# Picking silu and its product ahead of weight copies in the feed-forward parts of a two-layer decoder trunk

## The chip, the cores and the metric

The kernel runs on one core of one Trainium2 chip. The metric is the device time of one execution in microseconds (us). The core's engines are named as in the profile: PE does matrix products and PEld their weight loads, ACT the activations and copies, DVE the elementwise work, POOL a few small operations, and SP issues the loads from HBM.

## The reference

Two layers (D = 1024, 256 positions, so two tiles of 128 positions, called t = 0 and t = 1) each mix tokens by attention and then run a SwiGLU feed-forward part, all in float32. The change touches only the second half of each layer:

```
h = rms_norm(x, norm_ffn[l]) * (1.0 + sc_f) + sh_f
gt, up = jnp.split(h @ w_ffn_in[l], 2, axis=-1)
x = x + g_f * ((jax.nn.silu(gt) * up) @ w_ffn_out[l])
```

The inner width of the feed-forward part, D_FF, is 2816.

## The kernel before

Every float32 weight is used as two parts. A weight tile of 1 MB (128 x 2048) is loaded from HBM into a buffer called `raw`. ACT copies it with rounding into `hi`, DVE subtracts (`raw - hi`) into `lo`, and each product of activations with weights is then three matmuls on PE: hi by hi, hi by lo, lo by hi. There are three `raw` buffers for this stage, and three `hi` and three `lo`; a new copy into `hi` can start only when the last matmul that reads the buffer's old contents has been issued and done.

The feed-forward part (stage `ffn`, function `sublayer_ffn`) goes through D_FF in six blocks: five of 512 columns and one of 256. For each block and each t, PE gathers the gate sums in one bank of the matmul memory (tiles called `bank`) and the up sums in another. Then `post` runs: ACT takes silu of the gate bank into a `tmp` tile, DVE multiplies it by the up bank, PE transposes the product, and ACT and DVE split the transposed product into a high and a low part (`aT`). The silu frees the gate bank for new sums, the product frees the up bank. Six banks hold such sums. The second product (stage `fout`) follows: eleven tiles of `w_ffn_out` are loaded, split in the same way and multiplied with `aT` into four banks.

The order of instructions on each engine isn't written out by hand. `Program.order` plans it before the kernel is built: it walks through time with estimated costs, and among the operations that can start at about the same moment on an engine it picks the one of highest rank. The rank is the length of the work that hangs on the operation plus a boost; operations recorded inside `with R.ahead():` get 1000 on top on every engine but PE, which puts them before all others that are ready:

```
def rank(self, e):
    return self.level + self.boost + (FIRST if self.first and e != "PE" else 0.0)
```

The split of weights (`split_unit`, line 631 for the copies and line 583 for the subtractions) is recorded inside such a block, `post` is not. Where the plan expects PE to wait for over 1.4 us, `fill` puts matmuls with a tile of zeros (`zb`, line 456) into the wait; their result is not used. PE takes its instructions in the planned order, and so do ACT, DVE and SP.

Of the kernel before, what the change touches and what calls it, by code (L numbers as in the profile page):

```python
# [8 lines left out]
F32 = mybir.dt.float32  # L9
# [3 lines left out]
AF = mybir.ActivationFunctionType  # L13
ALU = mybir.AluOpType
# [93 lines left out]
def AP(x):  # L108
    return x.ap() if isinstance(x, Ref) else x


def cols(x):
    n = 1
    for d in AP(x).shape[1:]:
        n *= d
    return n
# [442 lines left out]
class Engines:  # L559
# [22 lines left out]
    def tt(self, out, a, b, op, engs=("DVE",)):  # L582
        self._vec(engs, cols(out), True, lambda v: v.tensor_tensor(AP(out), AP(a), AP(b), op=op), [a, b], [out])  # L583
# [31 lines left out]
    def act(self, out, a, func, scale=None, bias=None, accum=None, late=()):  # L615
        kw, reads = {}, [a]
        c = (0.17 if self._psum(a) else 0.215) + cols(out) / 1200
        if scale is not None:
            kw["scale"] = scale
            reads.append(scale)  # L620
            c += 0.08 if isinstance(scale, Ref) else 0.0
        if bias is not None:
            kw["bias"] = bias
            reads.append(bias)
            c += 0.08
        writes = [out]
        if accum is not None:
            kw["accum_out"] = accum
            writes.append(accum)
            c += 0.2  # L630
        op = self.p.op({"ACT": (c, [lambda: self.nc.scalar.activation(AP(out), AP(a), func,  # L631
                                                                      **{k: AP(x) for k, x in kw.items()})])},
                       reads + list(late), writes)
        if any(func in x for x in TABLES):
            op.func = func
# [32 lines left out]
    def tr(self, out, a, ident):  # L668
        self.p.op({"PE": (0.109, [lambda: self.nc.tensor.transpose(AP(out), AP(a), AP(ident))])}, [a, ident], [out])  # L669

    def dma(self, out, src, q="SP", least=60000):
        o = AP(out)
        n = SIZE[o.dtype]
        for d in o.shape:
            n *= d
        n = max(n, least)
        eng = {"SP": self.nc.sync, "POOL": self.nc.gpsimd}[q]
        return self.p.op({q: (0.43 if q == "SP" else 0.6, [lambda: eng.dma_start(AP(out), AP(src))])},  # L678
                         [src], [out], nbytes=n)
# [5 lines left out]


HALVED = 1
SPILL = [("kb",), ("kb",)]
SPILL_FIRST = True
ADA_PACE = [(1.5, 1.5, 1.0), (0.7, 0.7, 0.3)]  # L690
# [11 lines left out]
def trunk_kernel(tc, pools, A):  # L702
# [14 lines left out]
    R = Program(nc)  # L717
    E_ = Engines(R)
    tt, stt, ttr, ts, act, evac, mm, tr, dma = (E_.tt, E_.stt, E_.ttr, E_.ts, E_.act, E_.evac, E_.mm, E_.tr, E_.dma)
# [46 lines left out]
    def temp(n=512):  # L766
        return R.val("tmp", lambda a: a[:, :n])
# [54 lines left out]
    def ada_dot(w, col):  # L822
        stt(w, w, 0.5, crow, ALU.mult, ALU.mult, accum=col)
# [303 lines left out]
    def lead_in(bs, h, W):  # L1127
# [7 lines left out]
        def load(k):  # L1135
            adas[k] = R.val("sa")
            src = A["w_ada"][0, :2 * D].rearrange("(j k p) c -> p j k c", j=2, p=P)[:, :, k]
            dst = adas[k].rearrange("p (j c) -> p j c", j=2)
            for js in ((slice(0, 1), slice(1, 2)) if k < HALVED else (slice(0, 2),)):
                dma(dst.of(js.start)[:, js] if k < HALVED else dst, src[:, js])  # L1140
            raws[k] = R.val("raw", lambda a: a[:, :NC0])
# [44 lines left out]
        for k in range(KD):  # L1186
# [3 lines left out]
            for j in range(2):  # L1190
                ada_dot((adas[k].of(j) if k < HALVED else adas[k])[:, j * D:(j + 1) * D], mod.of(k)[:, j, k:k + 1])
            with R.ahead():
# [20 lines left out]
    def sublayer_mix(l, h):  # L1213
# [355 lines left out]
        else:  # L1569
# [10 lines left out]
            for t in range(NT):  # L1580
                post_grpA(t, b1[t], b2[t])
            dense(0, 512, spilled(post_qa, SP["qa"]) if "qa" in SPILL[l] else post_qa)
        PACE[0] = ADA_PACE[l][0]
        mlp()
        if l:
            dense(1304, 512, spilled(post_qb, SP["qb"]) if "qb" in SPILL[l] else post_qb)
        dense(1816, 512, spilled(post_kb, SP["kb"]) if "kb" in SPILL[l] else post_kb)
        dense(2328, 512, post_vb)
# [57 lines left out]
    def sublayer_ffn(l, h):  # L1646
        W = A["w_ffn_in"][l]
        R.stage = f"{l}ffn"
        aT = {t: [] for t in range(NT)}
        last = [None]  # L1650

        def post(t, n, bg, bu):
            th = temp(n)
            act(th, bg[:, :n], AF.Silu)
            tt(th, th, bu[:, :n], ALU.mult)
            bt = R.val("t")
            with R.burst():
                for k in range(n // P):
                    tr(bt[:, k * P:(k + 1) * P], th[:, k * P:(k + 1) * P], ident)
            if t == 0:  # L1660
                last[0] = R.val("aT", dt=F32R)
            hi, lo = (quarter(last[0], 2 * t + i, t, i)[:, :n] for i in range(2))
            act(hi, bt[:, :n], AF.Copy)
            tt(lo, bt[:, :n], hi.bitcast(F32), ALU.subtract)
            aT[t] += [(hi[:, j * P:(j + 1) * P], lo[:, j * P:(j + 1) * P]) for j in range(n // P)]

        PACE[0] = ADA_PACE[l][2]
        c0 = 0
        while c0 < DFF:
            n = min(512, DFF - c0)  # L1670
            kt = 2048 // n
            nu = KD // kt
            b = {}
            us = {}
            for w, i in ([("gu"[c], k) for c, k, t in FFN_TURNS if t == 0] if c0 == 0 else
                         [(w, i) for w in "gu" for i in range(nu)]):
                off = c0 + (DFF if w == "u" else 0)
                us[w, i] = load_unit(W[i * kt * P:(i + 1) * kt * P, off:off + n], kt, n, spare=c0 == 0)
            keys = [(w, i, t) for w in "gu" for i in range(nu) for t in range(NT)]
            if c0 == 0:  # L1680
                keys = [("gu"[c], i, t) for c, i, t in FFN_TURNS]
            for w, i, t in keys:
                if i == 0:
                    b[w, t] = R.val("n")
                part(b[w, t], h[t], us[w, i], i * kt, i == 0)
            for t in range(NT):
                post(t, n, b["g", t], b["u", t])
            c0 += n

        WO = A["w_ffn_out"][l]  # L1690
        R.stage = f"{l}fout"
        R.boost = 100.0 if l == L - 1 else 0.0
        gate(l, "g_f")
        R.boost = 0.0
        nu = KF // 2
        bs = {(t, c): R.val("n") for t in range(NT) for c in range(2)}
        us = []
        for i in range(nu):
            ada_pace(PACE[0])
            raw = R.val("raw")  # L1700
            dma(raw.rearrange("p (k n) -> p k n", k=2), WO[i * 256:(i + 1) * 256].rearrange("(k p) n -> p k n", p=P))
            us.append(split_unit(raw, 2, D, l < L - 1 and i >= nu - 4))
        nl = 3 if l == L - 1 else 4
        keys = [(i, t, k, c) for i in range(nu - nl) for t in range(NT) for k in range(2) for c in range(2)]
        full = (0, 512)
        keys = [(*key, full) for key in keys]

        parts = {(t, c): [full] for t in range(NT) for c in range(2)}
        if l == L - 1:
            parts[(NT - 1, 1)] = [(0, 256), (256, 512)]  # L1710
            keys += [(i, t, k, c, e) for t in range(NT) for c in range(2) for e in parts[(t, c)]
                     for i in range(nu - nl, nu) for k in range(2)]
        else:
            keys += [(i, t, k, c, full) for t in range(NT) for i in range(nu - nl, nu) for k in range(2) for c in range(2)]
        for i, t, k, c, (e0, e1) in keys:
            kk = 2 * i + k
            cs_ = slice(c * 512 + e0, c * 512 + e1)
            b = bs[(t, c)]
            if (e0, e1) != full:
                b = b.of(e0)[:, e0:e1]  # L1720

            R.boost = 20.0 * (4 - 2 * t - c) - e0 / 50 if l == L - 1 and i >= nu - nl else 0.0
            mm3(b, aT[t][kk], us[i].hi[:, k, cs_], us[i].lo[:, k, cs_], kk == 0)
        R.boost = 0.0
        hn = []
        if l < L - 1:
            log_soon(last)
        for t in range(NT):
            for c in range(2):
                if l < L - 1:  # L1730
                    resid(l, t, c, bs[(t, c)], ada[l]["g_f"])
                    continue
                for e0, e1 in parts[(t, c)]:
                    xx = resid(l, t, c, bs[(t, c)], ada[l]["g_f"], e0, e1)
                    dma(out[t * P:(t + 1) * P, c * 512 + e0:c * 512 + e1], xx)
            if l < L - 1:
                hn.append(h_chain(t, *modulation(l + 1, "m")))
        return hn
# [58 lines left out]
```

## Time and profile before

| what | value |
|---|---|
| median of 3 runs | 827.29 us (824.45 to 827.35) |
| the profiled execution's own time | 825.58 us |
| its span in the profile | 823.8 us |
| PE busy, share of the span | 98% |
| DVE busy | 70% |
| ACT busy | 50% |

The span is what the profile covers from the first instruction to the last; the profiled execution's own time lies 1.8 us above it. In rows of the timeline a line stands for neighbouring instructions of one kind: start, duration, engine, line, operation, result and operands, shapes, their number, and in brackets how long the engine stood idle ahead of them and what ended the wait. Buffer numbers are left out there. The ends of matmuls are modelled and overlap the next start, so the pace of PE is read from start to start.

### The profile page before, as it was taken

How to read it: one execution, taken by the hardware profiler on the slowest of the kernel's cores; microseconds unless marked ns; L12 is line 12 of the kernel's file. 1: busy time of each engine (PE TensorE's matmuls, PEld its weight loads, DVE VectorE, ACT ScalarE, POOL GpSimd, SP SyncE). 2: the span in 40 equal slices, each digit the busy share in tenths (PEclk: the TensorE clock that was granted, in tenths of full speed). 3: DMA queues.
4: the chain of work that ended last, by engine and by line, in shares of the span. 5: the costliest groups of instructions: out<-in, count | busy, mean ns of one | idle time of the engine just before them, and what ended most of it. 6: DMA issues, size and time to landing. Idle time of an engine off the chain costs nothing.

```text
span 823.8 us, 10564 instructions
## 1 busy us (share of the span) xinstructions
PE 807.9 (98%) x4008; PEld 611.3 (74%) x4008; DVE 580.3 (70%) x1025; ACT 410.7 (50%) x654; POOL 79.6 (10%) x75
## 2 busy tenths in 40 slices
PE   8999999999999999999999999999999999998997
PEld 4567656754878888888878877775487888886886
DVE  6879876777887878776888897775468353444544
ACT  5455366652673334533684647576257353342431
POOL 4703620000100000000000360000000000000000
PEclk9999999999999999999999999999999999999999
DMA  9967585449858887967854876340473545644341
GB/s 358 416 241 266 179 297 189 153 130 333 328 192 320 316 323 269 340 261 282 314 188 174 309 245 215 141 155 1 178 281 122 186 151 207 204 153 154 142 165 51
DMA packets 74018, 183.82 MB, mean 223 GB/s; under 512 B 4304, under 2 KB 9696, under 8 KB 73456
## 3 DMA queue, kind: packets, MB, share of 16 engines
q1 hardware_dynamic: 73920, 183.08, 61.6%
q8 instruction: 31, 0.51, 0.2%
q14 instruction: 19, 0.16, 0.1%
q0 software_dynamic: 48, 0.08, 0.0%
HBM read 182.10 MB, written 1.05 MB: 222 GB/s over the span
## 4 chain that ended last, share of the span: by engine, by line
PE 87%; DVE 4%; ACT 2%; DMA 2%; POOL 2%; issue 1%; SPq 0%; DVEq 0%; POOLq 0%; ACTq 0%
PE bank L662 76%; PE bank L648 6%; PE bank L669 5%; DMA rows<-in_rows 1%; DVE tmp L583 1%; ACT hi L631 1%; DMA raw<-in_w_out 1%; DVE lo L583 1%; POOL tmp L601 1%; DVE tmp L601 1%; ACT hp L631 1%; PE bank L456 0%; POOL tmp L583 0%; SPq L678 0%; POOL at L1430 0%
## 5 line engine op out<-in xcount | busy, mean ns | idle before, releaser
L662 PE MATMUL bank<-hi,hp 128*128 128x512 f32 (+2 forms) x1296 | 361.1, 385 | 2.2 <-DVE hp L583 1.5
L583 DVE TENSOR_TENSOR lo<-raw,hi 128x2048 fp32r<-128x2048 f32 (+2 forms) x107 | 240.4, 2261 | 113.6 <-ACT hi L631 112.9
L631 ACT ACTIVATE hi<-raw 128x2048 fp32r<-128x2048 f32 (+2 forms) x107 | 200.7, 1891 | 237.5 <-PE bank L662 194.6
L662 PEld LDWEIGHTS bank<-hi,hp 128*128 128x128 f32 x1296 | 234.9, 188 | 59.5 <-issue 7.0
L662 PE MATMUL bank<-lo,hp 128*128 128x512 f32 (+2 forms) x648 | 209.9, 383 | 0.3 <-DVE lo L583 0.2
L662 PEld LDWEIGHTS bank<-lo,hp 128*128 128x128 f32 x648 | 119.7, 188 | 24.7 <-issue 2.6
L589 DVE SCALAR_TENSOR_TENSOR aw<-aw,crow 128x1024 f32<-128x1024 f32 x80 | 96.1, 1220 | 8.5 <-DMA aw<-in_w_ada 8.4
L662 PE MATMUL bank<-hi,aT 128*128 128x512 f32 (+1 forms) x364 | 101.7, 387 | 0.0
L662 PEld LDWEIGHTS bank<-hi,aT 128*128 128x128 f32 x364 | 66.6, 188 | 13.2 <-ACT hi L631 0.5
L662 PE MATMUL bank<-raw,yy 128*128 128x512 f32 x128 | 58.7, 596 | 0.7 <-ACT yy L640 0.7
L662 PE MATMUL bank<-lo,aT 128*128 128x512 f32 (+1 forms) x182 | 58.3, 385 | 0.0
L662 PE MATMUL bank<-raw,hd 128*128 128x512 f32 (+1 forms) x112 | 49.6, 568 | 0.9 <-ACT hd L631 0.9
L662 PEld LDWEIGHTS bank<-raw,yy 128*128 128x128 f32 x128 | 23.0, 190 | 23.7 <-issue 21.8
L662 PE MATMUL bank<-hi,mT 128*128 128x512 f32 x128 | 39.9, 403 | 0.5 <-ACT hi L631 0.5
L669 PE MATMUL bank<-ident,tmp 128*128 128x128 f32 x256 | 37.5, 274 | 1.5 <-DVE tmp L984 0.9
L662 PEld LDWEIGHTS bank<-lo,aT 128*128 128x128 f32 x182 | 34.1, 188 | 6.2
L631 ACT ACTIVATE at<-at,nb,rqa 128x128 f32<-128x128 f32 (+1 forms) x64 | 34.2, 535 | 7.5 <-DVE nb L589 7.5
L669 PEld LDWEIGHTS bank<-ident,tmp 128*128 128x128 f32 x256 | 30.4, 140 | 10.0 <-issue 1.8
L595 DVE CUSTOM_DVE_ANT_0 at<-bank,maskf 128x128 f32<-128x128 f32 (+1 forms) x96 | 29.5, 352 | 11.3 <-PE bank L669 8.9
L662 PEld LDWEIGHTS bank<-raw,hd 128*128 128x128 f32 x112 | 20.6, 189 | 17.1 <-issue 13.4
L583 DVE TENSOR_TENSOR tmp<-tmp,bank 128x512 f32<-128x512 f32 (+1 forms) x24 | 15.1, 638 | 20.5 <-PE bank L662 20.5
L947 POOL TENSOR_TENSOR r<-r,mhalf 128x4 f32<-128x4 f32 x4 | 4.1, 1027 | 254.4 <-DVE r L601 254.4
(185 smaller groups left out, 752.4 us busy)
## 6 DMA issues: line engine op xcount, KB each, us to landing
raw<-in_w_ffn_in SPq DMA_DIRECT2D x44, 1024.0 KB, 6.3
aw<-in_w_ada SPq DMA_DIRECT2D x80, 512.0 KB, 5.7
raw<-in_w_in SPq DMA_DIRECT2D x30, 1024.0 KB, 5.2
raw<-in_w_ffn_out SPq DMA_DIRECT2D x22, 1024.0 KB, 4.9
raw<-in_w_out SPq DMA_DIRECT2D x8, 1024.0 KB, 6.7
raw<-in_w_in SPq DMA_DIRECT2D x8, 908.0 KB, 9.5
sa<-in_w_ada SPq DMA_DIRECT2D x7, 1024.0 KB, 12.2
raw<-in_w_up_nsa SPq DMA_DIRECT2D x4, 1024.0 KB, 6.3
```

The source lines that it names most:

```text
L583: self._vec(engs, cols(out), True, lambda v: v.tensor_tensor(AP(out), AP(a), AP(b), op=op), [a, b], [out])
L589: lambda v: v.scalar_tensor_tensor(AP(out), AP(a), AP(s), AP(b), op0=op0, op1=op1, **{k: AP(x) for k, x in kw.items()}),
L595: lambda v: v.tensor_tensor_reduce(AP(out), AP(a), AP(b), 1.0, init, op0, op1, AP(accum)),
L601: lambda v: v.tensor_scalar(AP(out), AP(a), AP(s1), AP(s2), op0=op0, **kw),
L631: op = self.p.op({"ACT": (c, [lambda: self.nc.scalar.activation(AP(out), AP(a), func, **{k: AP(x) for k, x in kw.items()})])}, reads + lis ...
L648: op = self.p.op({"PE": (cost, [lambda: self.nc.tensor.matmul(AP(out), AP(lhsT), AP(rhs), start=start, stop=stop)])}, [lhsT, rhs], [out])
L662: self.nc.tensor.matmul(AP(out), AP(lhsT), AP(rhs), start=first, stop=v.gone == v.terms)
L669: self.p.op({"PE": (0.109, [lambda: self.nc.tensor.transpose(AP(out), AP(a), AP(ident))])}, [a, ident], [out])
L947: E_.raw("POOL", 1.1 + 0.13 * n, lambda: nc.gpsimd.tensor_tensor(AP(r), AP(r), AP(mh), op=ALU.pow), [r, mhalf], [r])
```

## The change

Three parts of `post` are wrapped in `R.ahead(...)`, switched by a table of three numbers. Silu (first) and the product with the up sums (second) now carry the mark; the split of the transposed product (third) is recorded as before, since its number is 0. Nothing is added to or taken from what is computed.

```
+AHEAD = (1, 1, 0)
...
         def post(t, n, bg, bu):
             th = temp(n)
-            act(th, bg[:, :n], AF.Silu)
-            tt(th, th, bu[:, :n], ALU.mult)
+            with R.ahead(AHEAD[0]):
+                act(th, bg[:, :n], AF.Silu)
+            with R.ahead(AHEAD[1]):
+                tt(th, th, bu[:, :n], ALU.mult)
...
             hi, lo = (quarter(last[0], 2 * t + i, t, i)[:, :n] for i in range(2))
-            act(hi, bt[:, :n], AF.Copy)
-            tt(lo, bt[:, :n], hi.bitcast(F32), ALU.subtract)
+            with R.ahead(AHEAD[2]):
+                act(hi, bt[:, :n], AF.Copy)
+                tt(lo, bt[:, :n], hi.bitcast(F32), ALU.subtract)
```

The order of SP and POOL is the same before and after. ACT, DVE and PE change in two stretches: a little in layer 0, where a few neighbours swap, and from the last two blocks of layer 1's feed-forward part to the end. The place in layer 1 is shown here. Names are those of the program with a running number (so `hi_5354` of before and `hi_5359` of the change are the same copy of the same weight tile); `bank_65` holds the gate sums and `bank_63` the up sums of the last 512-column block for t = 0, `bank_68` and `bank_66` those for t = 1, `bank_67` and `bank_64` hold the gate sums of the 256-column block for t = 0 and t = 1. `hi_5297` is that block's gate weights, `hi_5354` its up weights, and `hi_5371` and `hi_5380` are the first two tiles of `w_ffn_out`.

On ACT, after the copy `hi_5297` of the 256-column block's gate weights, before and after (- and +):

```order
 L631 ACTIVATE hi_5297<-raw_5195 128x2048
-L631 ACTIVATE hi_5354<-raw_5259 128x2048
-L631 ACTIVATE hi_5371<-raw_5272 128x2048
-L631 ACTIVATE hi_5380<-raw_5329 128x2048
 L631 ACTIVATE tmp_79<-bank_65 128x512
+L631 ACTIVATE hi_5359<-raw_5259 128x2048
+L631 ACTIVATE hi_5378<-raw_5272 128x2048
+L631 ACTIVATE hi_5397<-raw_5329 128x2048
 L631 ACTIVATE tmp_76<-bank_68 128x512
 L631 ACTIVATE tmp_77<-bank_67 128x256
 L631 ACTIVATE tmp_75<-bank_64 128x256
```

The silu of `bank_65` moves ahead of three weight copies; the other three silus stay behind them.

On DVE at the same place:

```order
 L583 TENSOR_TENSOR lo_5307<-raw_5195,hi_5297 128x2048
-L583 TENSOR_TENSOR lo_5373<-raw_5259,hi_5354 128x2048
-L583 TENSOR_TENSOR lo_5382<-raw_5272,hi_5371 128x2048
-L583 TENSOR_TENSOR lo_5401<-raw_5329,hi_5380 128x2048
 L583 TENSOR_TENSOR tmp_79<-tmp_79,bank_63 128x512
+L583 TENSOR_TENSOR lo_5380<-raw_5259,hi_5359 128x2048
+L583 TENSOR_TENSOR lo_5402<-raw_5272,hi_5378 128x2048
+L583 TENSOR_TENSOR lo_5427<-raw_5329,hi_5397 128x2048
 L583 TENSOR_TENSOR tmp_76<-tmp_76,bank_66 128x512
```

The product that frees `bank_63` moves ahead of three low parts in the same way.

On PE at the same place before, with the semaphores that are waited for (of eleven pairs of weight load and matmul with zeros the first and the last stand):

```order
L662 MATMUL bank_67<-hi_5297,hp_4627 128x256
L669 MATMUL bank_69<-ident_95,tmp_75 128x128 x4
L456 LDWEIGHTS zb_109
L456 MATMUL bank_68<-zb_109 128x512 [waits Activation_49]
...
L456 LDWEIGHTS zb_109
L456 MATMUL bank_68<-zb_109 128x512
L662 MATMUL bank_65<-hi_5354,hp_4627 128x256
L662 MATMUL bank_65<-lo_5373,hp_4627 128x256 [waits DVE_49]
L662 MATMUL bank_65<-hi_5354,hp_4627 128x256 x2
L662 MATMUL bank_65<-lo_5373,hp_4627 128x256
L662 MATMUL bank_68<-hi_5354,hp_4725 128x256
```

And the same place after the change:

```order
L662 MATMUL bank_67<-hi_5297,hp_4627 128x256
L669 MATMUL bank_69<-ident_95,tmp_75 128x128 x4
L662 MATMUL bank_65<-hi_5359,hp_4627 128x256 [waits Activation_49]
L662 MATMUL bank_63<-hi_5359,hp_4725 128x256 [waits DVE_49]
L662 MATMUL bank_63<-hi_5359,hp_4725 128x256 x15
L662 MATMUL bank_65<-hi_5359,hp_4627 128x256 x2
L662 MATMUL bank_63<-lo_5380,hp_4725 128x256 [waits DVE_49]
L662 MATMUL bank_63<-lo_5380,hp_4725 128x256 x7
L662 MATMUL bank_65<-lo_5380,hp_4627 128x256 x2
```

The eleven matmuls with zeros are gone, and the up sums of the 256-column block for t = 1 (`hp_4725`) go into `bank_63`, which the product frees, where they went into `bank_68`, which a silu frees. Seven more matmuls into `bank_65` follow these rows (36 of 128x256 in all behind the transposes), and then the first matmul of stage `fout` into `bank_68` and, behind it, its low-part matmul with `lo_5402`, and those into `bank_67` and `bank_64`.

## Rows read from the trace of the kernel before

**Rows 1.** The page's part 1: the span, and PE's busy time and share.

```profile
span 823.8 us, 10564 instructions
PE 807.9 (98%) x4008; PEld 611.3 (74%) x4008; DVE 580.3 (70%) x1025; ACT 410.7 (50%) x654; POOL 79.6 (10%) x75
```

**Rows 2.** Waits of PE, 625 to 824 us: us in total, times, longest.

```profile
PE bank L456 <- ACT tmp L631: 3.6, 1, 3.6
PE bank L662 <- DVE hp L583: 0.4, 1, 0.4
```

**Rows 3.** Waits of PE, 230 to 424 us (layer 0's feed-forward part).

```profile
PE bank L662 <- DVE hp L583: 1.1, 1, 1.1
```

**Rows 4.** The chain that ended last, 735 to 760 us: start, us, what.

```profile
741.23 3.69 ACT hi L631 x2
744.92 0.98 ACT tmp L631 x2
...
745.94 4.00 PE bank L456 x11
```

**Rows 5.** Timeline of PE, 738.4 to 750.1 us.

```profile
740.61 0.64 PE L662 MATMUL bank<-hi,hp 128*128 128x512 f32 x3
...
741.21 0.60 PE L669 MATMUL bank<-ident,tmp 128*128 128x128 f32 x4
741.57 0.37 PE L662 MATMUL bank<-hi,hp 128*128 128x256 f32 x1
741.77 0.60 PE L669 MATMUL bank<-ident,tmp 128*128 128x128 f32 x4
745.94 4.00 PE L456 MATMUL bank<-zb 128*128 128x512 bf16 x11 [3.57 <-ACT tmp L631]
749.59 0.47 PE L662 MATMUL bank<-hi,hp 128*128 128x256 f32 x1
```

**Rows 6.** Timeline of PE, 718 to 770 us: the pace of matmuls.

```profile
736.17 1.41 PE L662 MATMUL bank<-lo,hp 128*128 128x256 f32 x10
737.42 0.40 PE L662 MATMUL bank<-hi,hp 128*128 128x256 f32 x2
...
764.96 2.79 PE L662 MATMUL bank<-hi,aT 128*128 128x512 f32 x11
767.59 1.52 PE L662 MATMUL bank<-lo,aT 128*128 128x512 f32 x6
768.95 1.07 PE L662 MATMUL bank<-hi,aT 128*128 128x512 f32 x4
```

**Rows 7.** Timeline of ACT, 625 to 830 us.

```profile
673.18 0.58 ACT L631 ACTIVATE tmp<-bank 128x512 f32<-128x512 f32 x1
...
739.40 5.51 ACT L631 ACTIVATE hi<-raw 128x2048 fp32r<-128x2048 f32 x3 [5.66 <-PE bank L662]
744.82 1.61 ACT L631 ACTIVATE tmp<-bank 128x512 f32<-128x512 f32 x4
746.31 1.10 ACT L631 ACTIVATE aT<-bank 128x512 fp32r<-128x512 f32 x2
762.99 3.72 ACT L631 ACTIVATE hi<-raw 128x2048 fp32r<-128x2048 f32 x2 [15.58 <-PE bank L662]
```

**Rows 8.** Timeline of DVE, 625 to 830 us.

```profile
733.78 2.29 DVE L583 TENSOR_TENSOR lo<-raw,hi 128x2048 fp32r<-128x2048 f32 x1 [3.14 <-ACT hi L631]
741.35 6.70 DVE L583 TENSOR_TENSOR lo<-raw,hi 128x2048 fp32r<-128x2048 f32 x3 [5.28 <-ACT hi L631]
747.97 1.28 DVE L583 TENSOR_TENSOR tmp<-tmp,bank 128x512 f32<-128x512 f32 x2
```

**Rows 9.** Stretches: busy us of each engine, then granted clock, DMA share, GB/s.

```profile
742.20:745.40 3.20, 0.17 (x2) 0.00 (x0) 3.20 (x2) 3.20 (x4) 0.00 (x0) 1.00 0.10 13
745.40:748.80 3.40, 2.86 (x7) 0.99 (x7) 3.40 (x4) 2.01 (x5) 0.00 (x0) 0.52 1.00 402
```

**Rows 10.** Instructions on tile raw, 735 to 800 us: the loads' time to landing.

```profile
DMA to landing us min/median/max: 4.8/4.8/6.9
```

**Rows 11.** Waits of PEld, 285 to 345 us (layer 0, last 512-column blocks).

```profile
PEld bank L662 <- ACT hi L631: 0.7, 4, 0.2
PEld bank L662 <- DVE lo L583: 0.4, 1, 0.4
```

## The prediction

> **What bounds the kernel now.** I read the page's busy times first: PE is busy for 807.9 of 823.8 us [rows 1], so PE's own work sets the time almost everywhere, and a change that only reorders ACT and DVE can gain only where PE stands still or does work that nobody needs. The waits of PE come next, over the two feed-forward parts that the change touches. In layer 0's the largest is 1.1 us, and it is for `hp`, the normalised input, which `post` has no part in [rows 3]. In layer 1's there is one of 3.6 us, for ACT's silu (`tmp`), on line 456, and one of 0.4 us, again for `hp` [rows 2]. Line 456 is the matmul with zeros: the plan had foreseen a wait here and filled it. So PE's loss at this place is more than 3.6 us, because the zeros are a loss too.
>
> The timeline of PE gives its full length [rows 5]. Four transposes start at 741.21 and the next matmul at 741.57, so four transposes hold PE for 0.36 us; the last four start at 741.77, and without a wait the next matmul would have started at 741.77 + 0.36 = 742.13. The first that does useful work starts at 749.59. PE loses 749.59 - 742.13 = 7.46 us, of which some 3.8 are the wait and some 3.6 the eleven matmuls with zeros. They ran slowly: between 745.4 and 748.8 the granted clock is 0.52, near the lower of its two levels (1.2 of 2.4 GHz), after PE had stood still, while from 742.2 to 745.4 it is still 1.00 [rows 9].
>
> The chain of waits names the cause: ahead of the zeros stand the second and third of three weight copies on ACT and then two silus [rows 4]. On ACT's own timeline the three copies start at 739.40, when PE releases their buffer, and the silus only at 744.82 [rows 7]; DVE then does three low parts and the products from 747.97 on [rows 8]. The banks that PE wants next are held by sums that wait for those silus.
>
> **The change, part by part.** No instruction is added, except that the eleven zero matmuls and their weight loads go. What moves in layer 1 is one silu, ahead of three copies on ACT, and one product, ahead of three low parts on DVE; SP's order does not change, so no DMA is moved. I follow the new order from 742.13, with durations of the old trace.
>
> ACT: `bank_65` gets its last matmul at the same moment that releases the first copy, since the same weight tile's last use ends both, so the silu can start at 739.40. A silu of 512 columns takes 0.58 us, and a copy (744.82 - 739.40) / 3 = 1.81 us [rows 7]. So the copies end at about 739.40 + 0.58 + 1.92 (one copy with its end, from 3.72 for two less 1.81) = 741.90, then 743.71 and 745.52, and the silu of `bank_68` by 746.0. The seven operations together take what they took, so the last of them ends at about 746.4, as before.
>
> DVE: the product needs the silu (739.98) and the last matmul into `bank_63`, one of the three that start at 740.61 and are over by 741.25 [rows 5]. It takes at most 0.68 us (1.28 for two, less the 0.6 step) [rows 8], so `bank_63` is free by 741.95. The low parts follow their copies at once; one lasts 2.29 and the step is (747.97 - 741.35) / 3 = 2.21 us [rows 8]. They end at about 744.24, 746.45 and 748.66, that is 0.6 us later than before.
>
> PE: matmuls of 128x256 step by (737.42 - 736.17) / 10 = 0.125 us, those of 128x512 by (768.95 - 767.59) / 6 = 0.227 [rows 6]. The first needs the first copy: wanted at 742.13, there at 741.90. The second needs `bank_63`: wanted at 742.25, free at 741.95. The twentieth needs the first low part: wanted at 742.13 + 19 x 0.125 = 744.50, there at 744.24. The 37th needs `bank_68`: wanted at 742.13 + 36 x 0.125 = 746.63, free at 746.0. The 38th needs the second low part: wanted at 746.86, there at 746.45. `bank_67` and `bank_64` follow at 747.1 and 747.3 against some 746.4, and the third low part is wanted near 751, there at 748.66. So every wait is met, by margins of 0.2 to 0.6 us at the tight places. The signal between engines is not in these numbers; the nearest row is small (the silus end at 744.92 + 0.98 = 745.90 and PE starts at 745.94 [rows 4]). I charge 0.3 us, with 0 as the one bound and, for the four tightest waits each missed by 0.4, 1.6 us as the other. The gain here is 7.46 - 0.3 = 7.2 us.
>
> Behind this place PE runs 7.2 us earlier and could outrun what it is fed. The later copies wait for PE and not for data: ACT stands idle for 15.58 us until PE frees the next buffer at 762.99 [rows 7], so copies move up with PE. After that release PE has, before, six matmuls of 0.227 and eight transposes (two times 0.36) to do, 2.08 us, while the copy takes 1.92; after the change it has eight matmuls and four transposes, 2.18 us. Nothing to charge; bounds 0 and 0.3 at each of four such places, 1.2 us. For the loads, a buffer comes free when its low part is done, the first now at 744.24; a load lands 4.8 us later, at most 6.9 [rows 10], so at 749 to 751, while its copy can start only when PE frees the `hi` buffer, 7.2 us before 762.99, at about 755.8. At least 4.7 us are spare.
>
> In layer 0 four transposes move up by nine matmuls, and one silu and one product swap with a neighbour. PE loses nothing to ACT or DVE there that a new order could give back beyond 0.7 + 0.4 us of weight loads that wait [rows 11], and the same is the nearest price of a new wait. I take 0, with bounds of -0.5 and +0.5.
>
> **A rule against it.** The silu now stands ahead of copies on one queue, and the product ahead of low parts; here both find their sums ready by 741.25, before the first copy is done [rows 5, 7]. The Trainium skill (TensorE: Matmul & The Clock Gate, Architectural detail) says that ACT and DVE are strict first-in first-out, so whatever stands behind a waiting instruction waits too. By that rule a silu or product picked before its sums are complete would hold three copies or three low parts, and PE with them; the trace before has no such case, and the second rival below is this mechanism.
>
> **The rivals.** *The place is only moved*: PE meets a new wait in the same stretch. For it speaks that the margins are 0.2 to 0.6 us and that all low parts come 0.6 us later; against it that the first `fout` matmuls have 4.5 us of work ahead of them (36 x 0.125). If the product of `bank_63` ends 3 us late, each low part behind it is late by the same, and the gain is 7.5 - 3 = 4.5 us: 821.9.
>
> *The time is given back later*, so that nothing is left: PE arrives at the `fout` tiles earlier and then waits for loads. It needs landings of 4.8 + 4.7 + 7.2, some 17 us, where the longest here is 6.9 [rows 10]. Then 826.4, the level of before.
>
> *Slower*: a new wait of a few us with no zeros behind it lets the clock drop, and now real matmuls run at the lower level instead of zeros. The trace shows a drop of 3.4 us after one wait [rows 9], which would cost 1.7 us; to end over 4.1 us above before, PE would have to run (7.2 + 4.1) x 2 = 23 us at that level behind it, with the wait added. That gives 831 or more. The Trainium skill (TensorE: Matmul & The Clock Gate, Part 1) has the lower level as the default that PE's own activity lifts; the drop behind the wait agrees [rows 9].
>
> **How the numbers follow.** The profiled execution took 825.58 us; less 7.2 that is 818.4. Its time lies 1.7 below the median of the three runs, 827.29, which would go to 820.1. The runs spread over 2.9 us, so I forecast the middle, 819.3 us. The likeliest case has gains between 7.46 + 0.5 = 8.0 and 7.46 - 1.6 - 0.5 = 5.4, on a base of 824.45 to 827.35: 816.5 to 822.0. To take in part of the first rival, the range goes up to 822.5. Chances: the stall goes and nothing takes its place 0.84, moved in part 0.09, given back 0.04, slower 0.03. A measurement of this kernel can tell 0.5% from no change, 4.1 us. Faster by more: 0.84 and two thirds of the second case, 0.90; within it 0.07; slower 0.03.
>
> **What would show it.** Right: no line-456 matmuls near 742 us, no PE wait over 0.5 us from there to the end, the clock at 1.00 throughout, a silu at 739.4 followed by three copies, the following copies still released by PE, and the last matmul some 7 us earlier. Wrong: a PE wait for a DVE `tmp` or `lo` near 742 to 747, ACT copies released by a DMA on `raw`, or a wait in layer 0 that was not there. Most likely to upset the forecast is a signal between engines that costs more than the margins.

## The result, and the profile after

The changed kernel takes 817.8 us (median; 817.18 to 818.79) and the kernel before, run beside it, 826.37 us (824.45 to 827.35): a ratio of 0.990, 95% interval 0.9877 to 0.9924. It is 8.6 us faster; forecast were 7.2 us and a time of 819.3 us. The profiled execution took 817.18 us, with a span of 815.4.

The page's part 1 after, beside [rows 1]: PE's busy time falls by 4.1 us and its share rises, and eleven matmuls are gone.

```profile
span 815.4 us, 10543 instructions
PE 803.8 (99%) x3997; PEld 610.0 (75%) x3997; DVE 580.2 (71%) x1025; ACT 410.3 (50%) x654; POOL 79.5 (10%) x75
```

Waits of PE after, 625 to 816 us (us in total, times, longest), beside [rows 2]: the one of 3.6 us is gone, nothing stands in its place, and the one for `hp` is left.

```profile
PE bank L662 <- DVE hp L583: 0.5, 1, 0.5
```

Timeline of PE after, at the place of [rows 5]: behind the last four transposes the first matmul with up weights starts 741.32 - 740.97 = 0.35 us later, which is the transposes' own time. Nineteen matmuls with `hi`, the low parts and the first matmul of stage `fout` (`aT`) follow without a gap.

```profile
740.97 0.60 PE L669 MATMUL bank<-ident,tmp 128*128 128x128 f32 x4
741.32 2.52 PE L662 MATMUL bank<-hi,hp 128*128 128x256 f32 x19
743.68 1.36 PE L662 MATMUL bank<-lo,hp 128*128 128x256 f32 x10
...
745.72 0.40 PE L662 MATMUL bank<-hi,aT 128*128 128x512 f32 x1
745.95 0.40 PE L662 MATMUL bank<-lo,aT 128*128 128x512 f32 x1
```

Timelines of ACT and of DVE after, at the places of [rows 7, 8]: one silu, released by PE, then three copies, then three silus; one product, then three low parts. PE still releases the copy that follows, at 755.01, which is 7.98 us before the 762.99 of [rows 7].

```profile
738.60 0.60 ACT L631 ACTIVATE tmp<-bank 128x512 f32<-128x512 f32 x1 [5.66 <-PE bank L662]
739.09 5.51 ACT L631 ACTIVATE hi<-raw 128x2048 fp32r<-128x2048 f32 x3
744.50 1.13 ACT L631 ACTIVATE tmp<-bank 128x512 f32<-128x512 f32 x3
745.50 1.10 ACT L631 ACTIVATE aT<-bank 128x512 fp32r<-128x512 f32 x2
755.01 3.74 ACT L631 ACTIVATE hi<-raw 128x2048 fp32r<-128x2048 f32 x2 [8.41 <-PE bank L662]
```

```profile
740.32 0.69 DVE L583 TENSOR_TENSOR tmp<-tmp,bank 128x512 f32<-128x512 f32 x1 [5.05 <-PE bank L662]
741.03 6.70 DVE L583 TENSOR_TENSOR lo<-raw,hi 128x2048 fp32r<-128x2048 f32 x3
```

The stretches of [rows 9] after (busy us of PE, PEld, DVE, ACT, POOL; granted clock, DMA share, GB/s): PE is busy throughout and the clock stays at its higher level.

```profile
742.20:745.40 3.20, 3.20 (x29) 3.20 (x28) 3.20 (x2) 3.20 (x5) 0.00 (x0) 1.00 0.15 32
745.40:748.80 3.40, 3.40 (x19) 2.87 (x18) 3.40 (x5) 1.21 (x3) 0.00 (x0) 1.00 1.03 423
```

Where the 8.4 us of span come from is read by splitting it at the start of the last four transposes, which stand in both traces: ahead of them 741.77 before and 740.97 after, from there to the end 823.8 - 741.77 = 82.03 before and 815.4 - 740.97 = 74.43 after. So 7.60 us are gained from this point on, and 7.47 of them between the transposes and the first useful matmul (749.59 - 741.77 = 7.82 against 0.35). The other 0.8 us lie ahead of the place. The second length (called the **tail** below) is what I compare between experiments, since the start of the transposes itself wanders from 740.85 to 743.04 us over the traces of all kernels here. A tail is that of one execution: the traced ones of `front_only` and `product_back` are the fastest of their kernels (820.78 and 825.67 us), those of `no_zeros` and `silu_back` the slowest (824.01 and 825.81 us), so where the two differ the medians count.

### The profile page after: what moved, and what is told of

The parts are those of the page before. It is cut to its first block, busy times and chain, and to the rows that moved or that the text cites. A ratio compares the mean times of both kernels' runs of the same rounds, so it can differ in the third digit from the quotient of the medians.

```text
span 815.4 us, 10543 instructions
## 1 busy us (share of the span) xinstructions
PE 803.8 (99%) x3997; PEld 610.0 (75%) x3997; DVE 580.2 (71%) x1025; ACT 410.3 (50%) x654; POOL 79.5 (10%) x75
## 4 chain that ended last, share of the span: by engine, by line
PE 88%; DVE 4%; DMA 2%; ACT 2%; POOL 2%; issue 1%; SPq 0%; DVEq 0%; POOLq 0%
PE bank L662 77%; PE bank L648 6%; PE bank L669 5%; DMA rows<-in_rows 1%; DVE tmp L583 1%; DMA raw<-in_w_out 1%; DVE lo L583 1%; POOL tmp L601 1%; DVE tmp L601 1%; ACT hp L631 1%; ACT hi L631 1%; SPq L678 0%; POOL tmp L583 0%; POOL at L1431 0%; DVE e L583 0%
## 5 line engine op out<-in xcount | busy, mean ns | idle before, releaser
L631 ACT ACTIVATE tmp<-bank 128x512 f32<-128x512 f32 (+2 forms) x43 | 20.7, 509 | 16.3 <-PE bank L662 7.0
```

## The experiments

My theory was that of the held bank: PE stops because the bank that it wants next holds sums whose silu or product stands behind three copies or low parts. Rivals were that the matmuls with zeros were the loss, that one half of the change (the places on ACT and DVE, or PE's order) is enough, and that layer 0 or the product's mark carries the gain. Times are medians. The experiments ran in three groups, each beside the kernel before on the same chip (825.84, 825.98 and 826.03 us), and the ratio is to that.

| kernel | us | ratio to before, 95% | tail, us |
|---|---|---|---|
| before | 826.37 | | 82.03 |
| the change | 817.8 | 0.9877 to 0.9924 | 74.43 |
| no_zeros | 822.7 | 0.9935 to 0.997 | 79.25 |
| front_only | 823.36 | 0.995 to 0.9978 | 77.72 |
| silu_back | 823.39 | 0.9962 to 0.9986 | 80.96 |
| product_back | 827.97 | 1.0005 to 1.003 | 83.05 |
| pe_only | 826.58 | 0.9996 to 1.0021 | 82.82 |
| zeros_back | 820.6 | 0.991 to 0.9949 | 76.75 |
| l1 | 818.48 | 0.9882 to 0.9918 | 74.41 |
| l0 | 826.07 | 0.9984 to 1.0015 | 83.16 |
| silu | 817.8 | 0.9888 to 0.9921 | 74.5 |
| prod | 826.39 | 0.9989 to 1.0013 | 82.02 |
| silu_early | 820.71 | 0.9925 to 0.9955 | 78.03 |

**Where the marks count.** Four kernels plan anew with fewer marks: `l1` and `l0` in one layer only, `silu` and `prod` on one operation only. The edit of `l1` is shown; `l0` has `l == 0` in its place.

```
-            with R.ahead(AHEAD[0]):
+            with R.ahead(AHEAD[0] and l == 1):
...
-            with R.ahead(AHEAD[1]):
+            with R.ahead(AHEAD[1] and l == 1):
```

> The mark only in layer 1: layer 0 keeps the order of before, layer 1 has that of the change. Theory of the held bank in layer 1: 818.2 us (817.5 to 819), so nearly all of the gain, short by the 0.3 us that layer 0's swap gave in the trace. Rival (the gain comes from the new order of layer 0 as much): 822 us or more.

> The mark only in layer 0: layer 0 has the order of the change, layer 1 that of before, with its zeros. Theory of the held bank in layer 1: 826.0 us (825.3 to 826.7). Rival (layer 0 gives a good part): 823 us or less.

```
-AHEAD = (1, 1, 0)
+AHEAD = (1, 0, 0)
```

> The mark on silu alone, not on the product. PE, ACT and SP get the order of the change; on DVE two products of 256 columns stand two places later than in the change, and the product of bank_63 stands ahead of the three low parts without the mark as well. Theory of the held bank: the whole gain, 817.8 us (817 to 818.7). Rival (both marks are needed): 822 us or more.

```
-AHEAD = (1, 1, 0)
+AHEAD = (0, 1, 0)
```

> The mark on the product alone, not on silu. PE, ACT and SP keep the order of before; on DVE two products of 256 columns stand two places earlier. A product can't be ready before its silu, and silu stays behind the copies: 826.4 us (825.7 to 827). Rival (the product's place carries the gain): 818 us.

All four came out at the theory's level: layer 1 alone and silu alone give the whole gain (tails 74.41 and 74.5), layer 0 alone and the product's mark alone nothing. The 0.3 us that I had given layer 0's new order in the first two expectations is not there. In the trace of before a weight copy waits for a load in that stretch, in the trace of `l1`, with the same old order of layer 0, it doesn't. Timeline of ACT before, layer 0:

```profile
298.87 3.72 ACT L631 ACTIVATE hi<-raw 128x2048 fp32r<-128x2048 f32 x2 [5.82 <-PE bank L662]
...
310.99 1.92 ACT L631 ACTIVATE hi<-raw 128x2048 fp32r<-128x2048 f32 x1 [0.84 <-DMA raw<-in_w_ffn_in]
...
321.52 3.72 ACT L631 ACTIVATE hi<-raw 128x2048 fp32r<-128x2048 f32 x2 [6.66 <-PE bank L662]
```

The same in `l1`:

```profile
299.16 3.72 ACT L631 ACTIVATE hi<-raw 128x2048 fp32r<-128x2048 f32 x2 [5.82 <-PE bank L662]
...
308.49 3.74 ACT L631 ACTIVATE hi<-raw 128x2048 fp32r<-128x2048 f32 x2 [4.65 <-PE bank L662]
...
321.45 3.72 ACT L631 ACTIVATE hi<-raw 128x2048 fp32r<-128x2048 f32 x2 [7.28 <-PE bank L662]
```

From pair to pair of copies that is 321.52 - 298.87 = 22.65 us before and 321.45 - 299.16 = 22.29 in `l1`; after the change it is 22.31. A load that came late in one execution cost 0.34 us there. Over layer 0's feed-forward part, from the matmul behind PE's wait for `hp` to the eight transposes of `gcol` near the end, before took 407.12 - 232.14 = 174.98 us and the change 406.27 - 231.90 = 174.37, but `l1`, with the old order, 407.02 - 232.63 = 174.39, and `l0`, with the new one, 406.25 - 231.74 = 174.51. So 0.6 of the 0.8 us that before lost ahead of the place belong to its one execution, and layer 0's new order shows no gain; by the interval of `l0`'s ratio the times show that to some 1.3 us.

**The zeros.** The next two take the planned order and edit it by hand: `no_zeros` drops the eleven matmuls with zeros from the order of before, `zeros_back` puts eleven into the order of the change, there into `bank_65`, which the silu has freed by then. (In these two and the five after them lines are added, so that lines 662, 669, 631 and 583 stand 40 to 49 lines lower in their rows, and the zeros of `zeros_back` are at line 594.)

```
+    def edited(self, out):
+        return [x for x in out if not (x[2].stage == "fill" and x[0] > 600)]
```

> The kernel before without the eleven matmuls with zeros of that place in layer 1; their result is used nowhere, and the order of everything else stays. Theory of the held bank: PE still waits for the silus behind the three copies, to about 745.9 us in the trace of before, so at most 7.5 - 3.8 = 3.7 us come back, less up to 1.7 if the clock drops and real matmuls run at the lower level: 822 to 825 us. Rival (the zeros themselves were the loss): 818 to 819 us. Here and for the other runs the levels are 826.4 us for before and 817.8 us for the change.

```
+        op = Op(-1, {"PE": (2.5, [lambda: self.nc.tensor.matmul(
+            bank.rearrange("p (a b) -> p a b", b=P), AP(zs), AP(zs)[:, None, :].to_broadcast([P, 4, P]),
+            start=True, stop=True)] * 11)}, 0.0)
+        op.stage = "fill"
+        return out[:at] + [(0.0, "PE", op)] + out[at:]
```

> The change, with eleven matmuls with zeros put back at the place where they stood (behind the last transposes, ahead of the first matmul of the next weight tile), where PE now has nothing to wait for. Theory of the held bank: they run at the full clock, some 0.22 us each, 2.4 us in all, and nothing else moves: 820.2 us (819.5 to 821). Rival (the zeros were the whole loss): 825 to 826 us.

Timeline of PE in `no_zeros`:

```profile
742.95 0.60 PE L709 MATMUL bank<-ident,tmp 128*128 128x128 f32 x4
746.63 0.58 PE L702 MATMUL bank<-hi,hp 128*128 128x256 f32 x1 [3.08 <-ACT tmp L671]
```

A stretch of `no_zeros` (busy us of each engine, then granted clock, DMA share, GB/s):

```profile
745.00:748.80 3.80, 2.17 (x10) 2.17 (x11) 3.80 (x2) 3.58 (x7) 0.00 (x0) 0.68 0.67 244
```

PE in `zeros_back`:

```profile
741.65 0.60 PE L718 MATMUL bank<-ident,tmp 128*128 128x128 f32 x4
742.08 2.54 PE L594 MATMUL bank<-zb 128*128 128x512 bf16 x11
744.27 2.62 PE L711 MATMUL bank<-hi,hp 128*128 128x256 f32 x19
```

Without zeros the wait stays, and the time lands in the theory's range, 3.1 us below before: PE starts to work 3.68 us after the transposes instead of 7.82, but now real matmuls bear the lower clock, 0.68 from 745.0 to 748.8 us. `zeros_back` is in its range too, 2.8 us above the change by the medians and 76.75 - 74.43 = 2.32 by the tails. Zeros without a wait take 744.27 - 742.08 = 2.19 us, where they took 749.59 - 745.94 = 3.65 in the stall [rows 5]. In the kernel before they filled no wait, since their own bank, `bank_68`, was the one that the silu had to free; they came behind it. The zeros are a part of the loss; without them the wait is still there.

**One half without the other.** `front_only` gives the kernel before, without zeros, the change's places on ACT and DVE and leaves PE's order; `pe_only` gives the change's order on PE and, at this place, leaves ACT and DVE as they were. Elsewhere `front_only` has the order of before and `pe_only` that of the change.

```
+        a[i - 3:i + 1] = [a[i]] + a[i - 3:i]
+        d[j - 3:j + 1] = [d[j]] + d[j - 3:j]
```

> The kernel before without those eleven zero matmuls, with the one silu put ahead of the three copies on ACT and the one product ahead of the three low parts on DVE, as in the change; PE keeps its order, so the next up sums for t = 1 still go into bank_68, whose silu stays behind the copies. Theory of the held bank: the place on ACT and DVE isn't enough by itself, PE must also be sent to the bank that is freed; it does six matmuls of 128x256 and then waits to about 745.9 us: 822 to 824 us. Rival (the places on ACT and DVE are all that matters, beside the zeros): 818 us.

```
+        d[j:j + 4] = d[j + 1:j + 4] + [d[j]]
+        q["ACT"][i:i + 4] = q["ACT"][i + 1:i + 4] + [q["ACT"][i]]
```

> The change's order on PE (no zeros, the next up sums for t = 1 into bank_63), with both the silu and the product of layer 1 put back behind copies and low parts, so that ACT and DVE have the order of before. Theory of the held bank: PE waits from about 741.4 us for the product of bank_63, which now stands behind its silu and behind three low parts, until about 748.4 us: 827 to 828.5 us, as with the product alone put back. Rival (PE's new order carries the gain, without the places on ACT and DVE): 818 to 820 us.

Timeline of PE in `front_only`, and then in `pe_only`:

```profile
741.63 0.36 PE L709 MATMUL bank<-hi,hp 128*128 128x256 f32 x1
743.69 0.39 PE L709 MATMUL bank<-lo,hp 128*128 128x256 f32 x1 [1.70 <-DVE lo L630]
...
745.44 0.39 PE L709 MATMUL bank<-hi,hp 128*128 128x256 f32 x1 [1.02 <-ACT tmp L678]
```

```profile
745.05 0.39 PE L708 MATMUL bank<-hi,hp 128*128 128x256 f32 x1 [3.08 <-ACT tmp L677]
748.30 3.99 PE L708 MATMUL bank<-hi,hp 128*128 128x256 f32 x17 [2.87 <-DVE tmp L629]
```

In `front_only` PE comes to its second matmul at once and needs the first low part, then waits a second time for the silu of `bank_68`, which stands behind the copies. The order of before has 29 short matmuls behind the transposes, five into `bank_65` and then 24 into `bank_68`; the sixteen of those that need only the `hi` part stand behind the first low part and the second silu, so they can't cover the time in which the low part is made. The time was in the range; my picture of six matmuls ahead of one wait was not. `pe_only` is level with before, 0.4 us under its range, with two waits in place of one. Against `no_zeros`, which has neither half, `front_only` is no faster by the medians and `pe_only` about 4 us slower; both halves together, the change, are some 5 us faster (822.7 against 817.8). Neither is enough alone: what `front_only` gains on before is no more than dropping the zeros gives.

**One place at a time.** `silu_back` and `product_back` are the change with one of the two put back, by one each of the two lines of `pe_only`.

> The change, with the one silu of layer 1 put back behind the three copies on ACT, and all else in the change's order (the product ahead of the low parts, no zeros). Theory of the held bank: PE waits for that silu from about 741.3 us of the trace after to 744.6 or later, and DVE's low parts stand behind the product that waits for it, so they come some 4 us late as well; with the clock's drop up to 1.7 us more: 822 to 826 us. Rival (the loss was the zeros, the silu's place is worth nothing): 818 us.

> The change, with the one product of layer 1 put back behind the three low parts on DVE, and all else in the change's order (the silu ahead of the copies, no zeros). Theory of the held bank: the bank of the up sums is freed only at about 748.4 us of the trace after, wanted at 741.4, so PE waits 6.9 us and may run up to 1.7 us slower behind it: 825 to 827 us. Rival (silu alone matters): 818 us.

Waits of PE in `silu_back`, 625 us to the end, and two stretches behind the transposes, which start at 743.04:

```profile
PE bank L705 <- ACT tmp L674: 3.1, 1, 3.1
PE bank L705 <- DVE hp L626: 0.5, 1, 0.5
```

```profile
745.00:748.80 3.80, 1.94 (x7) 1.65 (x8) 2.11 (x2) 3.67 (x7) 0.00 (x0) 0.66 0.02 4
748.80:752.00 3.20, 3.20 (x17) 3.20 (x16) 3.20 (x3) 0.00 (x0) 0.00 (x0) 0.50 0.25 73
```

The same in `product_back`, where the transposes start at 740.85, with the stretch ahead:

```profile
PE bank L707 <- DVE tmp L628: 6.7, 1, 6.7
PE bank L707 <- DVE hp L628: 0.5, 1, 0.5
```

```profile
741.20:745.00 3.80, 0.37 (x4) 0.17 (x2) 3.80 (x2) 3.80 (x4) 0.00 (x0) 1.00 0.19 16
745.00:748.80 3.80, 0.54 (x2) 0.54 (x3) 3.80 (x4) 1.49 (x4) 0.00 (x0) 0.54 0.98 395
748.80:752.00 3.20, 3.20 (x17) 3.20 (x16) 0.00 (x1) 0.00 (x0) 0.00 (x0) 0.50 1.03 402
```

Each place is needed. With the silu behind the copies the time is in its range and level with `no_zeros` (823.39 and 822.7): PE waits 3.1 us for `bank_65` as there, and then real matmuls run at the lower level. With the product behind the low parts the kernel is a little slower than before (ratio 1.0005 to 1.003), though it has no zeros: PE waits 6.7 us, and then too real matmuls run at the lower level. In the trace its tail is 83.05 - 74.43 = 8.6 us longer than the change's, the expected 6.9 and 1.7; the median, 2.3 us above the traced execution, is 1 us above the range that I had given it, and that part is not explained.

**A silu that is too early.** `silu_early` is the rule against the change made real: a second silu, that of `bank_67`, goes ahead of the three copies, though its sums are complete only just ahead of the last transposes.

```
+        a[i + 1:i + 6] = [a[i + 5]] + a[i + 1:i + 5]
```

> The change, with a second silu ahead of the three copies on ACT: that of bank_67, whose sums are complete only behind them in PE's order, at about 741.1 us of the trace after, while the copies' buffer is free at 738.6. If a queue waits behind its first instruction, the copies start at about 741.4 instead of 739.1 us, the first ends at 743.3, PE wants it at 741.3 and waits some 2 us: 819.8 us (819 to 820.8). Rival (the copies don't wait behind a silu that isn't ready, or the margin covers it): 817.8 us.

Timeline of ACT in `silu_early`, then of PE, then one stretch:

```profile
738.80 0.60 ACT L675 ACTIVATE tmp<-bank 128x512 f32<-128x512 f32 x1 [5.66 <-PE bank L706]
741.37 0.38 ACT L675 ACTIVATE tmp<-bank 128x256 f32<-128x256 f32 x1 [1.97 <-PE bank L706]
741.65 5.51 ACT L675 ACTIVATE hi<-raw 128x2048 fp32r<-128x2048 f32 x3
```

```profile
743.60 3.30 PE L706 MATMUL bank<-hi,hp 128*128 128x256 f32 x19 [1.83 <-ACT hi L675]
746.70 2.14 PE L706 MATMUL bank<-lo,hp 128*128 128x256 f32 x10
```

```profile
745.00:748.80 3.80, 3.80 (x22) 3.80 (x21) 3.80 (x3) 3.80 (x6) 0.00 (x0) 0.55 0.44 128
```

ACT stands idle for 1.97 us with three ready copies behind the silu, PE waits 1.83 us for the first of them, and behind this short wait the clock falls to 0.55. The nineteen matmuls take 746.70 - 743.60 = 3.10 us against 743.68 - 741.32 = 2.36 after the change, so the price is 2.9 us by the medians (3.6 by the tails) and not the 2.0 of the wait alone. The time, 820.71 us, lies just inside the range, but the expectation had left the clock out.

## Why the prediction was right, step by step

- **The stall and its length.** Right: 7.46 us were forecast for it, 7.47 went. That the bank held by a silu behind copies is its cause is shown by `silu_back` and `product_back`, where the wait comes back when the one place is put back, and that both the wait and the zeros count by `no_zeros` and `zeros_back`.
- **The new order meets every wait.** Right. The product starts at 740.32 and takes 0.69, so `bank_63` is free at 741.01, and the matmul that wants it starts some 0.12 us behind 741.32; the low parts start at 741.03. The charge of 0.3 us for signals did not appear: the gap behind the transposes is 0.35 us. This term was mis-sized, and measured 0.
- **Behind the place nothing is given back.** Right: from the first useful matmul to the end it is 823.8 - 749.59 = 74.21 us before and 815.4 - 741.32 = 74.08 after, and the copies that follow are still released by PE.
- **Layer 0 is worth nothing.** Right, by `l0` and `l1`. The traces of before and after alone would have told otherwise, in part by a load that came late once.
- **The base and the size.** The forecast of 819.3 was 1.5 us too high: 0.3 is the charge, 0.1 the base (826.5 taken, 826.37 measured), and 1.1 are left. That is within what the ratio's interval leaves open (0.0047 x 826 = 3.9 us from end to end), and `l1` gained 7.5 us. One likely cause can be seen: the stall's price was taken from one execution, and the granted clock behind it is not the same each time. In the trace of `l0`, with the order of before at this place, the clock is at 0.82 already from 741.2 to 745.0 us and still at 0.74 from 748.8 on, the eleven zeros took 749.39 - 745.10 = 4.29 us against 3.65, and the tail is 83.16 against 82.03, which makes the gain 8.7 us:

```profile
745.10 4.85 PE L456 MATMUL bank<-zb 128*128 128x512 bf16 x11 [3.56 <-ACT tmp L631]
749.39 0.78 PE L662 MATMUL bank<-hi,hp 128*128 128x256 f32 x1
```

```profile
741.20:745.00 3.80, 0.33 (x4) 0.16 (x2) 3.80 (x3) 3.80 (x5) 0.00 (x0) 0.82 0.23 51
745.00:748.80 3.80, 3.70 (x9) 1.31 (x9) 3.80 (x5) 1.57 (x5) 0.00 (x0) 0.50 1.02 406
748.80:752.00 3.20, 3.20 (x20) 2.74 (x19) 0.81 (x2) 0.00 (x0) 0.00 (x0) 0.74 1.00 351
```

Over the runs of before in the three groups of experiments, the 18 with a mean clock of 0.995 took 825.41 to 828.78 us and the 9 with 1.000 took 822.70 to 825.41 (medians 827.0 and 823.6), while all runs of the change timed against before for the result had 1.000. So the gain itself is some 6 us against the one kind and 9 against the other. That the fall at this stall makes this difference fits its direction but is not shown, since only one execution of each kernel has a trace. The trace that the forecast was made from has a mean clock of 0.998, between the two; that is luck, and it kept the forecast near.
- **The rule on queues.** The Trainium skill (TensorE: Matmul & The Clock Gate, Architectural detail) says that ACT and DVE take their instructions strictly in order. `silu_early` agrees, with 1.97 us of idle ACT ahead of three copies whose data and buffers were there. It doesn't speak against the change because the silu that the change moves has its sums ready. (The rival that the prediction calls the second here is the first of its three, *the place is only moved*.)
- **The rival "slower".** Its mechanism exists, its size was far off here: in `product_back`, the worst case, a wait of 6.7 us was followed by granted clocks of 0.54 and 0.50, and the tail ended 1.0 us above that of before. The Trainium skill (TensorE: Matmul & The Clock Gate, Part 1) has the lower level as the one an idle PE falls to, and these stretches agree.

## What to carry to other kernels

When PE waits for a bank, look at which short instruction frees it and at what stands ahead of that on its queue; here 0.6 us of silu and 0.7 of product behind three copies and three low parts cost 7.5 us. Moving it pays only if its input is complete by then and if PE's own order goes to the bank that is freed first: either half alone gained nothing beyond what dropping the zeros gives. Matmuls with zeros that themselves wait for a silu behind the copies fill nothing and lengthen the stall, here by some 3 us.

## What was not expected

The wait of only 1.83 us in `silu_early` was followed by 3.8 us at a granted clock of 0.55 with PE busy throughout, while in the traced execution of `front_only` two waits of 1.70 and 1.02 us left the clock at 1.00:

```profile
741.20:745.00 3.80, 1.53 (x12) 1.13 (x10) 3.77 (x3) 3.80 (x4) 0.00 (x0) 1.00 0.15 12
745.00:748.80 3.80, 3.36 (x26) 3.32 (x27) 3.80 (x4) 1.92 (x5) 0.00 (x0) 1.00 0.89 357
```

The runs of `front_only` show mean clocks from 0.995 to 1.000 and times from 820.78 to 824.31 us, so a short wait may well have one price in one execution and another in the next; one trace each can't show it, and what decides it these runs don't settle. In `product_back` the clock was still 1.00 for 3.8 us of waiting (741.2 to 745.0) before it fell, so that the lower level was paid mostly by the matmuls behind the wait.
